# One transpose for lambda's real and imaginary rows, and two products without a reader removed

## The chip, the cores and the metric

The kernel runs on one core of a Trainium2 chip. The metric is the device time of one execution in microseconds (us), and the figure for a kernel is the median over several executions. A core has these engines, each with its own queue of instructions that it works through in order: PE (TensorE, matrix products; its weight loads are listed apart as PEld), DVE (VectorE), ACT (ScalarE), POOL (GpSimd), and SP (SyncE, which here only issues DMA transfers). An instruction waits on semaphores until what it reads has been written and what it overwrites has been read.

## The reference, cut to what matters

One encoder layer on 512 tokens of 1024 features, all in float32. A normalised input is projected by `w_in`; part of it feeds a state-space branch (S5), part a gated mixing branch (gMLP); the two are merged by sigmoid gates. Cross-attention to 256 memory tokens and a SwiGLU feed-forward network follow, each with a residual.

```python
def s5_scan(u, lam_re, lam_im, log_step, b_re, b_im, c_re, c_im, reverse):
    lam = lax.complex(lam_re, lam_im)                 # (32 groups, 64 states)
    step = jnp.exp(log_step)[:, None]
    lam_bar = jnp.exp(lam * step)
    b_bar = ((lam_bar - 1.0) / lam)[..., None] * b
    ...
def reference(...):
    n = rms_norm(h, mix_norm_g[i]); proj = n @ w_in[i]
    ya = s5_branch(xa, ...)                           # forward and backward direction
    yb = sgu_branch(zu, zv, ...)                      # layer_norm(gelu(zv)), position mixing
    h = h + (gate_a * (ya @ w_proj_a) + gate_b * (yb @ w_proj_b)) @ w_out
    h = h + memory_cross_attention(rms_norm(h, ...), memn, w_q, w_k, w_v, w_xo)
    h = h + swiglu(rms_norm(h, ...), w_gate, w_up, w_down)
```

The parameters `s5_lam_re` and `s5_lam_im` have the shape (direction, group, state) = 2 x 32 x 64.

## The kernel before, in words

Every large product is made of three matmuls. A float32 matrix is split into a high part (a cast on ACT, L85, the tile `whi`) and a low part (a subtraction on DVE, L86, the tile `wlo`), and high x high, high x low and low x high are summed in PSUM. Weights come as blocks of 128 x 1024 elements: an SP transfer into `wraw`, the cast, the subtraction, then the matmuls; each of the three kinds of tile has three buffers. Products of the input projection are the rows `pt` (zv, the gated branch) and `pf` (other columns). In attention and feed-forward a quadrant scheme with pre-added weights is used; its products are the rows of `product` (L1258).

The state-space branch is side work: a Python generator, `s5_program`, yields what each step costs, and a credit that grows with the main products (`tick`) decides where the next step's code is put between them. What this case touches of it, in its order:

- `s5_setup` (from L692). `lam` comes in as 32 rows of 128 values (two directions of 64 states) for the real and the same for the imaginary part, and is turned on PE to 128 x 32 (L710, tile `plam` in PSUM), then copied by DVE into a slab of small tiles (L712). The rows of B and C are turned in four groups of four transposes (`pbc`, L733 and L741), copied by ACT to `raw_b` and `raw_c`. From `lam` and the step come the decay (Exp, L750), the angle, its reduction (L751 to L756), two Sin on ACT (L757, L758), and the powers (L766 to L780).
- `s5_kernels` (from L861) makes on DVE the factors `e0`, `e1` and on PE the convolution taps: a group `pk` (L894, L899) of 32 + 32 matmuls in a pinned order, into one bank.
- `s5_inputs` (from L946) makes on DVE the input factors (L980 to L984), which are turned (`pw`, L959), copied to `wt` by ACT (L960, two halves) and multiplied with the inputs `u` (`pz`, L966); ACT and DVE keep half of the result each (L971, L972).

Beside it runs `layer_norm` (from L1140) of the four token tiles of zv: DVE makes the mean `nm` (L1143, L1144), ACT two sums of squares (L500), DVE the variance `ms` (L1148, L1149), POOL its power -1/2 (`r`, L1150), DVE the product `nm` (L1151) and ACT the normalised tile `zt` (L1152). POOL's queue also carries weight transfers (L289, `bsum`).

Three things set the order. The code is written in an order that the credit decides; then a scheduler reorders each engine's instructions at build time with a simulated timeline (`schedule_with_timeline_sim`, L2024); and instructions wrapped in `in_order` keep the order in which they were written among each other. Small results in PSUM take turns in three banks (`aux`); the large accumulations have five (`bank`). `idle_product` (L1262) writes a 128 x 512 product into an `aux` bank that nothing reads; it is called once in attention (L1576) and once in the feed-forward network (L1775), each time inside `in_order`.

Of the kernel before, what the change touches and what calls it, by code (L numbers as in the profile page):

```python
# [9 lines left out]
F32 = mybir.dt.float32  # L10
# [7 lines left out]
P = 128  # L18
# [8 lines left out]
G = 32  # L27
# [25 lines left out]
def hybrid_layer_kernel(  # L53
# [8 lines left out]
    nc = tc.nc  # L62
    x, mem, out = x[0], mem[0], out[0]
# [13 lines left out]
    def bank(name):  # L77
        return pm.tile([P, 512], F32, tag="mm", name=name)

    def aux(name, shape=(P, 512)):  # L80
        return pa.tile(list(shape), F32, tag="aux", name=name)
# [12 lines left out]
    in_order = tc.keep_in_program_order  # L94
# [395 lines left out]
    ident = cp.tile([P, P], F32, name="ident")  # L490
# [73 lines left out]
    def token_slot(name, place=NEAR):  # L564
        return tuple(slot(tag, (P, KD, T), F32R, name, place) for tag in "BC")
# [3 lines left out]
    s5p = s5.enter_context(tc.tile_pool(name="s5", bufs=1))  # L569
# [119 lines left out]
    V = nc.vector  # L689
    lo_, hi_ = slice(0, 64), slice(64, 128)  # L690

    def s5_setup():  # L692
        A_ = nc.scalar
        slab = s5p.tile([P, 32, G], F32, tag="wt", name="slab", bufs=2)
        used = [0]

        def small():
            used[0] += 1
            return slab[:, used[0] - 1, :]
# [2 lines left out]
        for d in range(2):  # L702
            nc.sync.dma_start(ls[64 * d:64 * d + 64, :], s5_log_step[0, d].partition_broadcast(64))
        in_order(A_.activation(stp, ls, AF.Exp))
        lam = []
        lrows = s5p.tile([G, 2, 2, 64], F32, tag="etmp", name="lrows")
        for i, src in enumerate((s5_lam_re, s5_lam_im)):
            nc.sync.dma_start(lrows[:, i], src[0].rearrange("d g p -> g d p"))
            ps = aux("plam", (P, G))
            nc.tensor.transpose(ps, lrows[:, i].rearrange("g d p -> g (d p)"), ident[:G, :G])  # L710
            l = small()
            V.tensor_copy(l, ps)  # L712
            lam.append(l)
        lr, li = lam
        yield 0.3


# [12 lines left out]
        for n in range(2):  # L730
            ps = aux("pbc", (P, C // 4, P))
# [6 lines left out]
        for i in range(2):  # L738
            ps = aux("pbc", (P, C // 4, P))
# [319 lines left out]
    def s5_program():  # L1059
        yield from s5_setup()  # L1060
        for o in (2, 3):
            yield from s5_kernels(o)
        while "u" not in st:
            yield None
        zh = s5p.tile([P, NCH, 2, G], F32, name="zh")
        st["zh"] = zh
        for o in range(NO):
            yield from s5_inputs(o)
        for o in (0, 1):
            yield from s5_kernels(o)  # L1070
        while st.get("nz", 0) < 2 * NO:
            yield None
        yield None
        yield from s5_scan()
        for _ in range(2):
            yield None
        for o in range(NO):
            yield from s5_outputs(o)
# [129 lines left out]
    for h in range(H):  # L1208
        ps = bank("psv")
# [49 lines left out]
                                     stop=k == 3 and i == 2, skip_group_check=True)  # L1259
        tick(2.7)  # L1260

    def idle_product(x, y):  # L1262

        in_order(nc.tensor.matmul(aux("idle"), x[:, 0, 0:P], y[:, 4, :], start=True, stop=True))

    def unit_bank(name):
        return bank(name).rearrange("p (j t) -> p j t", j=2)

    def seed(x):
        v = unit_bank("qv")  # L1270
        nc.scalar.copy(v, x)
        return v
# [147 lines left out]
    hn_hi, hn_lo = token_slot("hn", AWAY)  # L1420
# [53 lines left out]
    def v_evac(half):  # L1474
        def f(t, ps):
# [10 lines left out]
    hops = {q: (hn_hi[:, ks, ts], hn_lo[:, ks, ts])  # L1486
            for q, ks, ts in ((1, K0, T0), (2, K1, T0), (7, K0, T1), (4, K1, T1))}
# [85 lines left out]
    qx, qq_ = unit_bank("qx"), None  # L1573
    query_product(qx, 0, 1, True)
    qv = seed(qx)
    idle_product(hops[1][0], hn_hi)  # L1576
    qq_ = unit_bank("qq")
    query_product(qq_, 0, 5, True)
    query_product(qv, 0, 2)
# [40 lines left out]
    fn_hi, fn_lo = token_slot("fn", AWAY)  # L1620
# [3 lines left out]
    ps = {t: bank(f"pt{t}") for t in range(NT)}  # L1624
# [45 lines left out]
    held, ps = [], {}  # L1670
# [70 lines left out]
    ops = {1: fn_q(K0, T0), 2: fn_q(K1, T0), 7: fn_q(K0, T1), 4: fn_q(K1, T1)}  # L1741
# [14 lines left out]
    def unit_second(u, v):  # L1756
        product(v, u, 2, False, ops)
        put(u, 0, T0, v)
# [3 lines left out]
    ps = [bank("pf0"), bank("pf1")]  # L1762
# [9 lines left out]
    begun = unit_start(UNITS[0])  # L1772
    gate_part(1, T0)
    unit_second(UNITS[0], begun[1])
    idle_product(ops[1][0], fn_hi)  # L1775
    for i in range(2):
        gate_part(i, T1)
    for j in range(2):
# [51 lines left out]
    for i, u in enumerate(UNITS):  # L1830
        final = i == len(UNITS) - 1
        x, v = begun
# [196 lines left out]
```

## Time and profile before

| | us |
|---|---|
| median of 3 executions (lowest, highest) | 863.52 (862.94, 864.19) |
| the profiled execution | 863.27 |
| its span, first to last instruction | 861.5 |
| outside the span | 1.77 |
| PE busy | 854.4 (99%) |
| weight loads (PEld) busy, beside PE | 765.6 (89%) |
| DVE busy | 662.8 (77%) |
| ACT busy | 465.2 (54%) |
| POOL busy | 89.2 (10%) |

A row of a timeline shows the start in us from the span's start, the duration in us, the engine, the line in the kernel, the operation, out<-in, the shape, how often it stands in a row (xN), and in brackets how long the engine was idle before it and which instruction ended that. A matmul's duration includes the way through the array, so it overlaps the next one; what it costs is the distance from its start to the next start. Plain float32 matmuls (transposes, `pk`, `pz`) are recorded as two passes each, so a group of eight shows as x16; transposes show once.

### The profile page before, as it was taken

The numbers are of one execution on the slowest core, as the hardware profiler recorded it, in microseconds if no ns is written. First come the engines' busy times: TensorE is split into PE (matmuls) and PEld (weight loads), VectorE is DVE, ScalarE is ACT, GpSimd is POOL, SyncE is SP. The second block draws the span as 40 slices with busy tenths as digits, with TensorE's granted clock in tenths as the row PEclk, the third lists the DMA queues.
The fourth block names the chain that finished last, engine by engine and source line by source line (L and its number), as shares of the span: only waits on it lengthen the run. The fifth ranks groups of instructions, "written<-read, shape, count | busy, mean of one in ns | idle before, by whom it ended". The sixth has DMA issues, their size and how long they took to land.

```text
span 861.5 us, 14748 instructions
## 1 busy us (share of the span) xinstructions
PE 854.4 (99%) x5768; PEld 765.6 (89%) x5768; DVE 662.8 (77%) x1079; ACT 465.2 (54%) x698; POOL 89.2 (10%) x119
## 2 busy tenths in 40 slices
PE   9999999999999999999999999999999999999997
PEld 6888888888889988899899888999999999988886
DVE  7699989899646867678758755867877768899876
ACT  6744763244455544457547544645545454655674
POOL 0002201211021110010010001000211111000000
PEclk9999999999999999999999999999999999999999
DMA  9759567987475798635696555557899898366564
GB/s 267 215 170 316 124 196 163 237 219 191 133 221 159 247 313 256 224 109 197 215 278 160 141 144 150 147 159 192 206 240 228 216 224 226 99 185 213 184 198 162
DMA packets 116200, 170.61 MB, mean 198 GB/s; under 512 B 9489, under 2 KB 80801, under 8 KB 116002
## 3 DMA queue, kind: packets, MB, share of 16 engines
q1 hardware_dynamic: 95778, 140.51, 49.9%
q0 software_dynamic: 20064, 28.55, 20.6%
q8 instruction: 45, 0.74, 0.3%
q10 hardware_dynamic: 288, 0.61, 0.2%
q14 instruction: 25, 0.20, 0.1%
HBM read 160.75 MB, written 48.73 MB: 243 GB/s over the span
## 4 chain that ended last, share of the span: by engine, by line
PE 99%; DVE 0%; ACT 0%; issue 0%
PE pf L374 27%; PE pt L374 18%; PE px L1258 13%; PE pq L1258 6%; PE dx L374 5%; PE dq L374 5%; PE pv L1258 3%; PE bx L1258 3%; PE qx L1258 3%; PE dv L374 2%; PE pz L966 2%; PE qv L1258 1%; PE po L374 1%; PE psc L374 1%; PE py L1022 1%; PE qq L1258 1%
## 5 line engine op out<-in xcount | busy, mean ns | idle before, releaser
L85 ACT CAST whi<-wraw 128x1024 fp32r<-128x1024 f32 x141 | 145.3, 1030 | 157.7 <-PE pf L374 52.3
L86 DVE TENSOR_TENSOR wlo<-wraw,whi 128x1024 fp32r<-128x1024 f32 x141 | 168.0, 1194 | 56.3 <-ACT whi L85 55.8
L374 PE MATMUL pf<-xn,whi 128*128 128x512 f32 x448 | 139.9, 392 | 0.0
L374 PEld LDWEIGHTS pf<-xn,whi 128*128 128x128 f32 x448 | 83.6, 188 | 17.2 <-issue 0.2
L374 PE MATMUL pf<-xn,wlo 128*128 128x512 f32 x224 | 87.7, 391 | 0.0
L1258 PE MATMUL px<-fn,whi 128*128 128x256 f32 x480 | 83.5, 277 | 0.0
L1258 PEld LDWEIGHTS px<-fn,whi 128*128 128x128 f32 x480 | 72.5, 188 | 0.2
L86 DVE TENSOR_TENSOR wlo<-b,whi 128x1024 fp32r<-128x1024 f32 x40 | 48.9, 1222 | 26.0 <-ACT whi L85 26.0
L85 ACT CAST whi<-b 128x1024 fp32r<-128x1024 f32 x40 | 42.2, 1054 | 47.9 <-PE px L1258 27.7
L1258 PE MATMUL px<-fn,wlo 128*128 128x256 f32 x240 | 66.4, 277 | 0.0
L1258 PE MATMUL pq<-s,whi 128*128 128x256 f32 x320 | 55.0, 276 | 0.0
L86 DVE TENSOR_TENSOR wlo<-t,whi 128x1024 fp32r<-128x1024 f32 x30 | 36.7, 1224 | 19.5 <-ACT whi L85 19.5
L85 ACT CAST whi<-t 128x1024 fp32r<-128x1024 f32 x30 | 31.6, 1054 | 36.2 <-PE pv L1258 13.3
L374 PEld LDWEIGHTS pf<-xn,wlo 128*128 128x128 f32 x224 | 42.1, 188 | 8.6
L1258 PEld LDWEIGHTS pq<-s,whi 128*128 128x128 f32 x320 | 48.1, 188 | 0.0
L1258 PEld LDWEIGHTS px<-fn,wlo 128*128 128x128 f32 x240 | 45.1, 188 | 0.0
L374 PE MATMUL pt<-whi,xn 128*128 128x512 f32 x128 | 44.4, 405 | 0.0
L1258 PE MATMUL pq<-s,wlo 128*128 128x256 f32 x160 | 44.2, 276 | 0.0
L374 PE MATMUL dx<-whi,s 128*128 128x512 f32 x132 | 41.4, 390 | 0.0
L374 PE MATMUL dq<-whi,s 128*128 128x512 f32 x122 | 38.1, 389 | 0.0
L289 POOL DMA_DIRECT2D dsum<-in_w_down_dram x12 | 13.2, 1103 | 171.2 <-DMA dsum<-in_w_down_dram 167.6
L500 ACT ACTIVATE sq<-h 128x512 f32<-128x512 f32 x23 | 14.5, 630 | 29.3 <-DVE h L1448 24.1
(458 smaller groups left out, 2243.3 us busy)
## 6 DMA issues: line engine op xcount, KB each, us to landing
wraw<-in_w_in_dram SPq DMA_DIRECT2D x34, 512.0 KB, 4.8
dsum<-in_w_down_dram SPq DMA_DIRECT2D x20, 512.0 KB, 6.0
wraw<-dsum SPq DMA_DIRECT2D x20, 512.0 KB, 3.9
b<-in_w_gate_dram SPq DMA_DIRECT2D x15, 512.0 KB, 6.2
b<-in_w_up_dram SPq DMA_DIRECT2D x15, 512.0 KB, 5.1
wraw<-in_w_down_dram SPq DMA_DIRECT2D x15, 512.0 KB, 4.5
dsum<-in_w_down_dram POOLq DMA_DIRECT2D x10, 512.0 KB, 7.7
dsum<-dsum POOLq DMA_DIRECT2D x10, 512.0 KB, 8.7
```

What stands on the lines that cost most here:

```text
L85: hi = nc.scalar.copy(dst_hi, src)
L86: lo = nc.vector.tensor_tensor(dst_lo, src, dst_hi.bitcast(F32), ALU.subtract)
L289: plan[j + step][1].append((0, lambda d=dst, x=more: nc.gpsimd.dma_start(d, x, accum_op=ALU.add)))
L374: m = nc.tensor.matmul(ps, a[x], b[y], start=start and i == 0, stop=stop and i == 2, skip_group_check=free)
L500: act = nc.scalar.activation(sq[:, :src.shape[-1]], src, AF.Square, bias=bias, accum_out=dst)
L966: nc.tensor.matmul(ps[:, g, :], wt[:, g, :], u[:, o * GO + g, :], start=True, stop=True)
L1022: in_order(nc.tensor.matmul(ps[64 * j:64 * j + 64, :, :, h, :].rearrange("p q d c -> p d q c"), a, b, start=k == ks[0], stop=k == ks[2], t ...
L1258: nc.tensor.matmul(ps[:, j, :], a[x], b[y], start=start and j == k == i == 0, stop=k == 3 and i == 2, skip_group_check=True)
```

## The change

First, the two parts of `lam` are loaded below each other into one tile of 64 rows x 128 values, turned by one transpose to 128 x 64 and copied by one DVE instruction into two neighbouring small tiles. The two transfers stay, with the same sizes. Second, `idle_product` and its two calls go.

```diff
--- before.py
+++ after.py
@@ -702,16 +702,13 @@
         for d in range(2):
             nc.sync.dma_start(ls[64 * d:64 * d + 64, :], s5_log_step[0, d].partition_broadcast(64))
         in_order(A_.activation(stp, ls, AF.Exp))
-        lam = []
-        lrows = s5p.tile([G, 2, 2, 64], F32, tag="etmp", name="lrows")
+        lrows = s5p.tile([2 * G, 2, 64], F32, tag="etmp", name="lrows")
         for i, src in enumerate((s5_lam_re, s5_lam_im)):
-            nc.sync.dma_start(lrows[:, i], src[0].rearrange("d g p -> g d p"))
-            ps = aux("plam", (P, G))
-            nc.tensor.transpose(ps, lrows[:, i].rearrange("g d p -> g (d p)"), ident[:G, :G])
-            l = small()
-            V.tensor_copy(l, ps)
-            lam.append(l)
-        lr, li = lam
+            nc.sync.dma_start(lrows[G * i:G * i + G], src[0].rearrange("d g p -> g d p"))
+        ps = aux("plam", (P, 2, G))
+        nc.tensor.transpose(ps.rearrange("p i g -> p (i g)"), lrows.rearrange("r d p -> r (d p)"), ident[:2 * G, :2 * G])
+        lr, li = small(), small()
+        V.tensor_copy(slab[:, used[0] - 2:used[0], :], ps)
         yield 0.3
 
 
@@ -1259,10 +1256,6 @@
                                      stop=k == 3 and i == 2, skip_group_check=True)
         tick(2.7)
 
-    def idle_product(x, y):
-
-        in_order(nc.tensor.matmul(aux("idle"), x[:, 0, 0:P], y[:, 4, :], start=True, stop=True))
-
     def unit_bank(name):
         return bank(name).rearrange("p (j t) -> p j t", j=2)
 
@@ -1573,7 +1566,6 @@
     qx, qq_ = unit_bank("qx"), None
     query_product(qx, 0, 1, True)
     qv = seed(qx)
-    idle_product(hops[1][0], hn_hi)
     qq_ = unit_bank("qq")
     query_product(qq_, 0, 5, True)
     query_product(qv, 0, 2)
@@ -1772,7 +1764,6 @@
     begun = unit_start(UNITS[0])
     gate_part(1, T0)
     unit_second(UNITS[0], begun[1])
-    idle_product(ops[1][0], fn_hi)
     for i in range(2):
         gate_part(i, T1)
     for j in range(2):
```

The lines after the first place are numbered 3 lower in the changed kernel, those behind the removed function lower still. The numbers behind names (buffers) shift by 3 as well.

Since the scheduler works over the whole program, the order of each engine differs in many places between 25 and 110 us, and in few behind. Three of them are shown, first before and then after the change.

ACT in the setup of the state-space branch (`slab` holds the small tiles: rows L704, L750/L747 are Exp, L757/L758 and L754/L755 the Sin; `raw_b` and `raw_c` are the copies of the turned B and C). Before:

```order
L704 ACTIVATE slab_337<-slab_337 128x32
L750 ACTIVATE slab_337<-slab_337 128x32
L85 CAST whi_381<-wraw_191 128x1024
L85 CAST whi_466<-wraw_379 128x1024
L734 COPY raw_b_360<-pbc_361 128x4x2x64
L734 COPY raw_b_360<-pbc_373 128x4x2x64
L85 CAST whi_472<-wraw_464 128x1024
L742 COPY raw_c_391<-pbc_392 128x4x128
L757 ACT_TABLE_LOAD
L757 ACTIVATE slab_337<-slab_337 128x32
L758 ACTIVATE slab_337<-slab_337 128x32
L1097 ACT_TABLE_LOAD
```

After:

```order
L704 ACTIVATE slab_337<-slab_337 128x32
L747 ACTIVATE slab_337<-slab_337 128x32
L754 ACT_TABLE_LOAD
L754 ACTIVATE slab_337<-slab_337 128x32
L755 ACTIVATE slab_337<-slab_337 128x32
L85 CAST whi_378<-wraw_191 128x1024
L731 COPY raw_b_357<-pbc_358 128x4x2x64
L85 CAST whi_463<-wraw_376 128x1024
L731 COPY raw_b_357<-pbc_370 128x4x2x64
L739 COPY raw_c_388<-pbc_389 128x4x128
L85 CAST whi_469<-wraw_461 128x1024
L739 COPY raw_c_388<-pbc_395 128x4x128
```

The load of the Sin table and the two Sin have moved ahead of three casts of weight blocks and the copies of B and C.

PE at the second group of convolution taps (`pt` are products of the input projection, `pk` the taps, `pw` turned input factors), the two parts before:

```order
L374 MATMUL pt2_783<-wlo_704,xn_137 128x512
L374 MATMUL pt2_783<-whi_703,xn_138 128x512
L894 MATMUL pk_741<-e0_613,bd0_519 32x128 x4
L374 MATMUL pt3_784<-whi_703,xn_137 128x512
L374 MATMUL pt3_784<-wlo_704,xn_137 128x512
```

```order
L374 MATMUL pt0_781<-whi_788,xn_138 128x512
L894 MATMUL pk_741<-e1_695,bd1_520 32x128 x4
L899 MATMUL pk_741<-e0_613,bd0_519 16x16 x4
L899 MATMUL pk_741<-e1_695,bd1_520 16x16 x4
L894 MATMUL pk_741<-e0_613,bd0_519 32x128 x4
L894 MATMUL pk_741<-e1_695,bd1_520 32x128 x4
L899 MATMUL pk_741<-e0_613,bd0_519 16x16 x4
L899 MATMUL pk_741<-e1_695,bd1_520 16x16 x4
L959 MATMUL pw_877<-ident_95,wsx_336 128x128 x4
```

After:

```order
L374 MATMUL pt1_779<-whi_700,xn_138 128x512
L891 MATMUL pk_738<-e0_610,bd0_516 32x128 x4
L891 MATMUL pk_738<-e1_692,bd1_517 32x128 x4
L896 MATMUL pk_738<-e0_610,bd0_516 16x16 x4
L896 MATMUL pk_738<-e1_692,bd1_517 16x16 x4
L891 MATMUL pk_738<-e0_610,bd0_516 32x128 x4
L891 MATMUL pk_738<-e1_692,bd1_517 32x128 x4
L896 MATMUL pk_738<-e0_610,bd0_516 16x16 x4
L896 MATMUL pk_738<-e1_692,bd1_517 16x16 x4
L374 MATMUL pt1_779<-whi_700,xn_137 128x512
L374 MATMUL pt1_779<-wlo_701,xn_137 128x512
```

The group stood in two parts with nine `pt` products between them, and stands in one piece now.

ACT where the layer norm and the inputs of the state-space branch meet (`squares` are the sums of squares, `zt` with L1097/L1094 the Gelu of zv, with L1152/L1149 the normalised tile, `wt` the turned factors, `zh` the kept halves of `pz`). Before:

```order
L500 ACTIVATE squares_1026,ss_1083<-zt_334,nm_1082 128x512 x2
L500 ACTIVATE squares_1026,ss_1131<-zt_334,nm_1130 128x512 x2
L1097 ACTIVATE zt_334,zsum_335<-pt2_783 128x512
L85 CAST whi_904<-wraw_895 128x1024
L960 COPY wt_975<-pw_976 128x512
L960 COPY wt_975<-pw_982 128x512
L971 COPY zh_829<-pz_988 64x8x64
L1097 ACTIVATE zt_334,zsum_335<-pt3_784 128x512
L85 CAST whi_1039<-wraw_902 128x1024
L1152 ACTIVATE zt_334<-zt_334,nm_1082,r_1085 128x1024
L1152 ACTIVATE zt_334<-zt_334,nm_1130,r_1133 128x1024
L971 COPY zh_829<-pz_1013 64x8x64
```

After:

```order
L500 ACTIVATE squares_1023,ss_1128<-zt_334,nm_1127 128x512
L1094 ACTIVATE zt_334,zsum_335<-pt2_780 128x512
L1149 ACTIVATE zt_334<-zt_334,nm_1079,r_1082 128x1024
L85 CAST whi_901<-wraw_892 128x1024
L957 COPY wt_972<-pw_973 128x512
L500 ACTIVATE squares_1023,ss_1223<-zt_334,nm_1222 128x512 x2
L957 COPY wt_972<-pw_979 128x512
L1149 ACTIVATE zt_334<-zt_334,nm_1127,r_1130 128x1024
L968 COPY zh_826<-pz_985 64x8x64
L1094 ACTIVATE zt_334,zsum_335<-pt3_781 128x512
L85 CAST whi_1036<-wraw_899 128x1024
L1149 ACTIVATE zt_334<-zt_334,nm_1222,r_1225 128x1024
```

The first `zt` of L1149, which waits for POOL's first `r`, now stands ahead of the cast of `whi_901` and of the two halves of `wt_972` (before: behind the corresponding `whi_904` and `wt_975`, and behind `whi_1039`).

PE's user of that `wt`, before:

```order
L374 MATMUL pf0_1035<-xn_138,whi_897 128x512
L374 MATMUL pf0_1035<-xn_137,wlo_898 128x512
L374 MATMUL pf0_1035<-xn_137,whi_897 128x512
L966 MATMUL pz_1013<-u_543,wt_975 128x64 x8
L374 MATMUL pf0_1035<-xn_138,whi_897 128x512
```

After:

```order
L374 MATMUL pf0_1032<-xn_138,whi_894 128x512
L374 MATMUL pf0_1032<-xn_137,wlo_895 128x512
L963 MATMUL pz_1010<-u_540,wt_972 128x64 x4
L374 MATMUL pf0_1032<-xn_137,whi_894 128x512
L374 MATMUL pf0_1032<-xn_138,whi_894 128x512
L374 MATMUL pf0_1032<-xn_137,wlo_895 128x512
L374 MATMUL pf1_1033<-xn_137,whi_894 128x512
L963 MATMUL pz_1010<-u_540,wt_972 128x64 x4
L374 MATMUL pf1_1033<-xn_138,whi_894 128x512
```

The group `pz` that reads it stood in one piece behind five `pf` products, and stands in two halves behind nine now.

## The prediction

> **What bounds the kernel now.** I read the page first, then PE's waits, then PE's timeline at each place that the change touches, then what feeds PE there. The page:
>
> ```profile
> PE 854.4 (99%) x5768; PEld 765.6 (89%) x5768; DVE 662.8 (77%) x1079; ACT 465.2 (54%) x698; POOL 89.2 (10%) x119
> ...
> PEclk9999999999999999999999999999999999999999
> ...
> PE 99%; DVE 0%; ACT 0%; issue 0%
> ```
>
> All waits of PE in the whole execution:
>
> ```profile
> PE pt L577 <- DVE ones L493: 1.1, 1, 1.1
> PE ptr L639 <- issue: 0.2, 1, 0.2
> PE ptr L639 <- DVE ms L622: 0.2, 1, 0.2
> ```
>
> PE carries 99% of the chain of waits, and its three waits (1.5 us) lie in the start. Everything behind is one unbroken row of matmuls at a constant granted clock, so two things move the time: PE work that is taken out counts in full, and every new wait of PE counts in full. DVE, ACT and POOL matter only where they make PE wait.
>
> **The two products without a reader.** PE's timeline at both places:
>
> ```profile
> 428.72 0.40 PE L1264 MATMUL idle<-hn 128*128 128x512 f32 x1
> 428.96 0.40 PE L1258 MATMUL qq<-hse,whi 128*128 128x256 f32 x2
> ...
> 548.91 0.39 PE L1264 MATMUL idle<-fn 128*128 128x512 f32 x1
> 549.14 1.07 PE L374 MATMUL pf<-fn,s 128*128 128x256 f32 x8
> ```
>
> From start to next start they cost 0.24 and 0.23 us: -0.47. They fill no gap: the products behind them (`qq`, `pf`) have no wait in the list above and their operands are weights and activations of long before, so nothing slides into the hole. In the feed-forward network the new order also puts five products of `w_up` ahead of a unit product; this only swaps equal work. Bounds: 0 (if the next product had needed those 0.23 us) to -0.47; I take -0.47.
>
> **The transposes of lambda.** PE around the first, and the transfers that feed both:
>
> ```profile
> 23.67 0.40 PE L374 MATMUL pt<-whi,xn 128*128 128x512 f32 x1
> 24.00 0.24 PE L710 MATMUL plam<-ident,lrows 32*128 32x32 f32 x1
> 24.17 0.50 PE L374 MATMUL pt<-whi,xn 128*128 128x512 f32 x1
> 24.51 0.39 PE L374 MATMUL pt<-wlo,xn 128*128 128x512 f32 x1
> 24.74 0.63 PE L374 MATMUL pt<-whi,xn 128*128 128x512 f32 x2
> ```
>
> ```profile
> L708 SPq DMA_DIRECT2D lrows<-in_s_lam_im_dram x1: 327/327/327, 9.3 to 9.3; - x1
> DMA to landing us min/median/max: 7.4/7.4/7.4
> ```
>
> A 512-column matmul takes 0.23 (24.51 to 24.74). From 23.67 to 24.51 there are two of them and one transpose: 0.84 - 0.46 = 0.38 for the transpose, most of it the two changes of kind, not its columns. The joint one has 64 columns instead of 32: its columns are part of the 0.17 from 24.00 to 24.17, so at most 0.17 more (0.55), at least nothing more (0.38). Two at 0.38 go, one comes: -0.38 to -0.21; I take -0.37, since nearly all of the 0.38 lies in the neighbours. It needs both transfers, but the later one was issued at 9.3 and lands by 16.7, and the transpose keeps its place at about 24.0: no wait.
>
> **What the new order does on PE.** The second group of taps `pk` stood in two parts and stands in one. PE at the two parts, and at a group in one piece:
>
> ```profile
> 71.01 0.39 PE L374 MATMUL pt<-whi,xn 128*128 128x512 f32 x1
> 71.33 0.42 PE L894 MATMUL pk<-e,bd 128*32 128x128 f32 x8
> 71.68 0.50 PE L374 MATMUL pt<-whi,xn 128*128 128x512 f32 x1
> 72.02 0.39 PE L374 MATMUL pt<-wlo,xn 128*128 128x512 f32 x1
> ...
> 73.63 0.39 PE L374 MATMUL pt<-whi,xn 128*128 128x512 f32 x1
> ...
> 74.94 1.09 PE L959 MATMUL pw<-ident,wsx 128*128 128x128 f32 x8
> ...
> 145.42 0.61 PE L374 MATMUL pf<-xn,whi 128*128 128x512 f32 x2
> ...
> 147.17 0.50 PE L374 MATMUL pf<-xn,wlo 128*128 128x512 f32 x1
> 147.51 0.62 PE L374 MATMUL pf<-xn,whi 128*128 128x512 f32 x2
> ```
>
> Part one: 72.02 - 71.01 - 0.46 = 0.55. Part two: 74.94 - 73.63 - 0.23 = 1.08. Whole: 147.51 - 145.42 - 3 x 0.23 = 1.40. Saved: 0.23. Elsewhere about as many groups `pz` and `pw` are split as are joined; at 0.1 per change of kind (0.34 instead of 0.23 at 147.17) I take 0, with 0.2 to either side.
>
> PE work in all: -0.47 - 0.37 - 0.23 = -1.07 us.
>
> **What the new order does to the feeders.** The two Sin and their table now stand ahead of the casts. Two idle times of DVE come from the old order, a third from a store:
>
> ```profile
> 33.67 1.23 DVE L86 TENSOR_TENSOR wlo<-wraw,whi 128x1024 fp32r<-128x1024 f32 x1 [1.37 <-ACT whi L85]
> ...
> 36.20 0.22 DVE L769 TENSOR_TENSOR pows<-slab 128x32 f32<-128x32 f32 x1 [1.31 <-ACT slab L757]
> ...
> 79.51 1.22 DVE L870 TENSOR_TENSOR e<-raw_c,pe 128x1024 f32<-128x1024 f32 x1 [1.38 <-DMA ed<-e]
> ```
>
> ```profile
> 27.91 1.05 ACT L85 CAST whi<-wraw 128x1024 fp32r<-128x1024 f32 x1 [1.88 <-PE pt L374]
> ```
>
> ACT was idle for 1.88 before its cast at 27.91; the table and the Sin fit about there, so the casts are not late for PE, and DVE gains 1.37 + 1.31 = 2.68 us. By itself that is worth nothing, since DVE is off the path. But DVE's lead lets the scheduler put the layer norm forward, and there is an operation that takes long once:
>
> ```profile
> L1150 POOL TENSOR_TENSOR r<-ms,mhalf x4: 542/548/3804, 91.6 to 107.6; 128x1 f32<-128x1 f32 x4
> ```
>
> ```profile
> 87.73 1.17 POOL L289 DMA_DIRECT2D bsum<-in_w_proj_b_dram  x1 [3.47 <-DMA bsum<-in_w_proj_b_dram]
> 91.61 4.33 POOL L1150 TENSOR_TENSOR r<-ms,mhalf 128x1 f32<-128x1 f32 x2 [2.71 <-DVE ms L1149]
> ...
> 95.45 0.16 DVE L1151 TENSOR_TENSOR nm<-nm,r 128x1 f32<-128x1 f32 x1 [0.46 <-POOL r L1150]
> ```
>
> ```profile
> 86.24 0.71 ACT L500 ACTIVATE squares<-zt,nm 128x512 f32<-128x512 f32 x1
> ...
> 88.93 1.03 ACT L85 CAST whi<-wraw 128x1024 fp32r<-128x1024 f32 x1
> 89.87 1.05 ACT L960 COPY wt<-pw 128x512 f32<-128x512 f32 x2
> ...
> 95.65 2.38 ACT L1152 ACTIVATE zt<-zt,nm,r 128x1024 f32<-128x1024 f32 x2 [1.98 <-DVE nm L1151]
> ```
>
> ```profile
> 92.36 1.89 PE L966 MATMUL pz<-u,wt 128*128 128x64 f32 x16
> ...
> 98.74 1.04 PE L959 MATMUL pw<-ident,wsx 128*128 128x128 f32 x8
> ```
>
> POOL's first `r` takes 3.80 us, the others 0.55. Before, ACT copied the two halves of `wt` at 89.87, and the first `zt` stood behind them, at 95.65. Now `zt` stands ahead of a cast and of both `wt` halves that PE's next `pz` reads. When does that `r` start? DVE has one sum of 1.14 us, a few small rows and one copy less ahead of it (1.3), and 2.68 of idle time less: 91.61 - 4.0 = 87.6. If the 1.38 at 79.51 goes too, 86.2. The transfer ahead of it on POOL (87.73 to 88.90) must have moved as well; paced by the same lead of about 2 us it ends near 86.9, and I take 86.9. Then `zt` starts 4.04 later (91.61 to 95.65), takes 1.19, the cast 0.94, the half `wt` 0.57: ready at 93.6 (92.9 to 94.3). PE reaches its `pz` after four more 512-column products and less the 0.60 saved till then: 92.36 + 0.91 - 0.60 = 92.7. New wait: 0.2 to 1.6, and 0.9 by the start that I take. The second half of `wt` follows 2.0 later (two squares at 0.71 and a copy), and PE's second half 1.8 later: no further wait of note. DVE stands still behind its `nm` for about 2.6 us, with two sums and a low part queued behind it; that eats the lead, and the `pw` that reads them is due only at 98.7.
>
> The Trainium skill, "GPSIMD Engine Reference", Instruction dispatch, puts the first call of a freshly loaded POOL kernel at approximately 6 us above its normal time. By that figure, as an estimate, `r` would take 2.7 us longer than the row says and the time would come to about 865.9; the trace has 3.80 for it, and that is used.
>
> **The sum.** -1.07 + 0.9 = -0.17 against the profiled 863.27, so 863.1; the profiled execution lies 0.25 below the median of the runs: 863.3 as a median.
>
> **Rivals.**
> 1. No new wait: `r` starts by 85.9, or the scheduler's order leaves ACT in time. -1.07: 862.4. For it: PE had no wait anywhere behind the start. Against it: 3.80 us now stand ahead of a copy that had 2.5 us of slack (89.87 to 92.36).
> 2. Slower, by the same `r`: if DVE's lead does not reach the layer norm (the 2.68 are lost again at the store of 79.51 or behind POOL's transfers), `r` starts only 1.2 earlier, at 90.4, and `wt` comes at 97.1: PE waits 4.4, +3.3, 866.8. It decides from a start at 88.8, where the wait passes 2.8. For it: POOL's transfer before had itself waited 3.47. The Trainium skill, "TensorE: Matmul & The Clock Gate", The HAM clock gate, has the TensorE clock halved after an idle window of about 3.4 us; by that, as an estimate, such a wait would be followed by some 3.4 us at half speed, +1.7, and no run here shows it, since the granted clock has no slice below 9 tenths. The removed products fill no gap, so at their own places it cannot start.
> 3. The removed work was hidden and nothing changes: 863.5. Against it: PE's starts follow each other without a gap.
>
> **How the numbers follow.** A difference under 0.2% (1.7 us) is about what a measurement cannot tell from none. My forecast (waits of 0.2 to 1.6) 0.50; rival 1 0.22; rival 3 0.04; rival 2 0.16; other new waits in the reordered stretch from 25 to 110 us, for +2 to +3 in all, 0.08. Faster by 1.7 needs more than all the PE work that I can find, so only a lucky spread of rival 1 (runs lie 0.6 apart) gets there: 0.08. Slower: 0.16 and three quarters of 0.08, 0.22. Same: 0.70. The range goes from 861.8 (rival 1 less the spread) to 865.5, which leaves rival 2 out and takes the smaller new waits in; the likeliest alone has 862.6 to 864.1.
>
> **What would show it.** In the changed kernel: no `idle` rows, one `plam` row; start-to-start across it 0.38 to 0.55 above the two matmuls; `pk` at 65 to 75 us with one part less; first `r` near 86.9 and again about 3.8 long; in PE's waits one new line `pz` <- ACT `wt` of about 0.9 near 93. A list as short as before means rival 1; `pz`, `pw` or `pf` lines over 2.8 us together mean rival 2. The prediction is wrong if PE work fell by another sum than about 1.1, or if waits arise anywhere outside 84 to 110 us.

## The result

The changed kernel took 869.92 us (median of 6, 868.61 to 872.76), the kernel before beside it 863.8 (median of 6, 862.94 to 866.37): a ratio of 1.0071, 95% interval 1.0054 to 1.0088. It is slower by some 6 us. Forecast were 863.3, with a range up to 865.5 and a chance of 0.22 for slower.

The page of the changed kernel, the lines that answer to those shown of before:

```profile
PE 860.9 (99%) x5765; PEld 772.7 (89%) x5765; DVE 663.7 (76%) x1078; ACT 464.5 (53%) x698; POOL 86.0 (10%) x119
...
PEclk9999999999999999999999999999999999999999
...
PE 93%; DMA 3%; DVE 2%; ACT 1%; issue 0%; POOL 0%; SPq 0%; ACTq 0%; DVEq 0%
```

All waits of PE in it (line, what for: total us, times, longest):

```profile
PE pt L577 <- DVE ones L493: 1.1, 1, 1.1
PE pt L374 <- DVE wlo L86: 0.3, 1, 0.3
PE ptr L639 <- DVE xt L633: 0.3, 1, 0.3
PE ptr L639 <- issue: 0.2, 1, 0.2
PE ptr L639 <- DVE ms L622: 0.2, 1, 0.2
```

The waits grew by 0.6 us. PE has three instructions less (5765 against 5768), and is busy 6.5 us longer (860.9 against 854.4) at the same granted clock. So it is not waits: the same products take longer. (That the chain leaves PE for 7% means only that it was followed back through the 0.3 us wait for a weight block.) Groups of PE's products between 549 and 742 us, first before, then after:

```profile
L1258 PE MATMUL px<-fn,whi 128*128 128x256 f32 x432 | 74.5, 276 | 0.0
L1258 PE MATMUL px<-fn,wlo 128*128 128x256 f32 x216 | 59.6, 276 | 0.0
```

```profile
L1255 PE MATMUL px<-fn,whi 128*128 128x256 f32 x432 | 77.3, 281 | 0.0
L1255 PE MATMUL px<-fn,wlo 128*128 128x256 f32 x216 | 60.7, 281 | 0.0
```

The second number from the end is the mean duration in ns: every group of 256-column products of this stretch has 281 where it had 276. Where that begins is seen at the place of the removed product. PE there, before:

```profile
548.20 0.40 PE L1258 MATMUL pv<-fn,whi 128*128 128x256 f32 x2
548.44 0.28 PE L1258 MATMUL pv<-fn,wlo 128*128 128x256 f32 x1
...
548.91 0.39 PE L1264 MATMUL idle<-fn 128*128 128x512 f32 x1
549.14 4.13 PE L374 MATMUL pf<-fn,s 128*128 128x256 f32 x35
```

And after:

```profile
548.98 0.40 PE L1255 MATMUL pv<-fn,whi 128*128 128x256 f32 x2
549.21 0.28 PE L1255 MATMUL pv<-fn,wlo 128*128 128x256 f32 x1
549.33 3.93 PE L374 MATMUL pf<-fn,s 128*128 128x256 f32 x32
```

Before the product, one 256-column product follows the other after 0.118 us (548.20 to 548.91 for six; two rows are left out). Behind it the step is (4.13 - 0.28) / 34 = 0.113 us. Without it, the step stays (3.93 - 0.28) / 31 = 0.118. Some 1,700 such products stand between 549 and 742 us (1,703 in PE's list). Over the whole stretch the mean step is 113.3 ns before (549.14 to 742.26, 1,704 steps) and 117.8 after (549.33 to 749.44, 1,699 steps), and 1,704 x 0.0044 = 7.5 us. That is more than the whole loss; the rest of the change had gained something. In the text below the two are called the 113 step and the 118 step.

### The profile page after: what moved, and what is told of

Its sections match the earlier page's. It is cut to its first block, busy times and chain, and to the rows that moved or that the text cites. A ratio compares the mean times of both kernels' runs of the same rounds, so it can differ in the third digit from the quotient of the medians.

```text
span 868.6 us, 14740 instructions
## 1 busy us (share of the span) xinstructions
PE 860.9 (99%) x5765; PEld 772.7 (89%) x5765; DVE 663.7 (76%) x1078; ACT 464.5 (53%) x698; POOL 86.0 (10%) x119
## 4 chain that ended last, share of the span: by engine, by line
PE 93%; DMA 3%; DVE 2%; ACT 1%; issue 0%; POOL 0%; SPq 0%; ACTq 0%; DVEq 0%
PE pf L374 23%; PE pt L374 16%; PE px L1255 13%; PE pq L1255 7%; PE dx L374 5%; PE dq L374 5%; PE pv L1255 3%; PE bx L1255 3%; PE qx L1255 3%; PE dv L374 2%; DMA wraw<-in_w_out_dram 2%; PE pz L963 2%; PE qv L1255 1%; PE po L374 1%; PE psc L374 1%; PE py L1019 1%
## 5 line engine op out<-in xcount | busy, mean ns | idle before, releaser
L1255 PE MATMUL px<-fn,whi 128*128 128x256 f32 x480 | 86.2, 281 | 0.0
L1255 PE MATMUL pq<-s,whi 128*128 128x256 f32 x320 | 57.0, 281 | 0.0
```

The lines of the kernel that those rows point to most:

```text
L1255: nc.tensor.matmul(ps[:, j, :], a[x], b[y], start=start and j == k == i == 0, stop=k == 3 and i == 2, skip_group_check=True)
```

## The experiments

**Each part alone.** First, the changed kernel with the feed-forward product put back; second, the kernel before without only that product; third, without only the attention product; fourth, the kernel before with only the joint transpose. The edits, of the first against the changed kernel and of the others against the kernel before:

```diff
# feed-forward product back
     unit_second(UNITS[0], begun[1])
+    idle_product(ops[1][0], fn_hi)
# feed-forward product gone
-    idle_product(ops[1][0], fn_hi)
# attention product gone
-    idle_product(hops[1][0], hn_hi)
# lambda only: the first hunk of the change
```

> The changed kernel with the feed-forward product without a reader put back (same place, 512 columns), nothing else. Theory A (this product switches the following row of 256-column products from 118 to 113 ns per product, some 1700 of them): 862.5 to 863.2, slots of 113 ns from about 549 us on. Theory B (the new order in the state-space stretch and its late weights cost the time): stays at 869 to 870, slots whatever they are. Theory C (each of the two products keeps a part of PE quick): about half way, 866.

Measured: 863.23 us (12 executions) against 864.6 (31 executions of the kernel before), ratio 0.9985, interval 0.9965 to 1.0006.

> The kernel before with only the feed-forward product without a reader taken out. Theory A: 870.5 to 871.5 (863.8 - 0.2 + 7.5), slots of 118 ns from 549 us on. Theory B: 863.5. Theory C: 866 to 867.

Measured: 872.47 us (6) against the same 864.6, ratio 1.0082, interval 1.0055 to 1.0108. (The ratios here are those on record; they differ a little from the quotient of the two medians, which is 1.0091 here.)

> The kernel before with only the attention product without a reader taken out. Theory A: 863.5, since PE's slots at its place are 113 ns before it and behind it. Theory B: 863.5. Theory C: 866 to 867.

Measured: 863.89 us (12), ratio 0.9986, interval 0.9969 to 1.0003.

> The kernel before with only the joint transpose of lambda (and the order that follows from it). Theory A: 863.0 to 863.4 (863.8 - 0.37 - 0.23, less what small waits take). Theory B: 869 to 870, since the whole reordering of the state-space stretch comes with this part. Theory C: 863.2.

Measured: 863.05 us (12), ratio 0.9982, interval 0.996 to 1.0003.

The feed-forward product alone carries the loss, in both directions: back in, the 6 us are gone; taken out of the kernel before, 8 us appear. The attention product and the joint transpose with its whole new order cost nothing; all three kernels that keep the feed-forward product lie 0.14% to 0.18% below the kernel before, with intervals that just reach past 1. Theories B and C fall. PE between 560 and 740 us in the second of them shows the same groups as in the changed kernel:

```profile
L1258 PE MATMUL px<-fn,whi 128*128 128x256 f32 x426 | 76.3, 281 | 0.0
```

and in the first as before:

```profile
L1255 PE MATMUL px<-fn,whi 128*128 128x256 f32 x432 | 74.5, 276 | 0.0
```

**What about the product does it.** Three kernels with the product back, but 384, 256 and 128 columns wide, one execution each:

```diff
-        in_order(nc.tensor.matmul(aux("idle"), x[:, 0, 0:P], y[:, 4, :], start=True, stop=True))
+        in_order(nc.tensor.matmul(aux("idle")[:, :n], x[:, 0, 0:P], y[:, 4, 0:n], start=True, stop=True))
```

> As the kernel with the feed-forward product put back, but 384 columns wide instead of 512. Theory A1 (the product works because it lasts longer than a weight load, so that the next load gets ahead of its matmul): slots of 113 ns from 549 us on, about 863. Theory A2 (any product more at this place shifts the phase): 113 ns too. Theory A3 (only a full bank of 512 columns does it): 118 ns, about 870.

> The same with 256 columns, the width of its neighbours. A1: 118 ns from 549 us on, about 870, since it lasts no longer than the others. A2: 113 ns, about 863. A3: 118 ns, about 870.

> The same with 128 columns. A1: 118 ns from 549 us on, about 870; a shorter product lets the loader fall further behind. A2: 113 ns, about 863. A3: 118 ns, about 870.

Measured: 862.34, 869.81 and 862.3 us (the kernel before beside them: 867.25, one execution, so only the steps are compared). PE behind the product of 384, of 256 and of 128 columns, in this order:

```profile
547.94 0.34 PE L1261 MATMUL idle<-fn 128*128 128x384 f32 x1
548.12 4.13 PE L374 MATMUL pf<-fn,s 128*128 128x256 f32 x35
```

```profile
548.11 0.28 PE L1261 MATMUL idle<-fn 128*128 128x256 f32 x1
548.23 4.05 PE L374 MATMUL pf<-fn,s 128*128 128x256 f32 x33
```

```profile
548.03 0.22 PE L1261 MATMUL idle<-fn 128*128 128x128 f32 x1
548.09 3.08 PE L374 MATMUL pf<-fn,s 128*128 128x256 f32 x25
```

4.13 for 35 is the 113 step, 4.05 for 33 the 118 step. The 25 products behind the narrow one begin with some at the longer step and go over within a microsecond (3.08 - 0.28 = 2.80 for 24, which is 0.117 on average, with one long step at the start); the groups behind have 276 ns. All three theories were wrong as put: it is not the length (128 does it too), not one product more (256 does not do it), not the full bank (384 does it). What works at this place is a product of another width than its neighbours; the one of 256 columns, written to PSUM in the same way, changes nothing.

**Does the state hold, and does the place matter?** The product of 512 columns, after the two parts of the gate product that follow:

```diff
     for i in range(2):
         gate_part(i, T1)
+    idle_product(ops[1][0], fn_hi)
```

> The product of 512 columns, but four parts of the gate product later (48 products of 256 columns and more behind its old place). If the state holds until something switches it: 118 ns up to the new place and 113 ns behind it up to about 742 us, 0.2 to 0.4 us more than with the old place, about 863.5. If the old place itself mattered: 118 ns throughout, about 870.

Measured: 864.91 us in one execution, with 1.0 us of waits of `pz` for ACT in it. PE at the new place:

```profile
554.82 1.34 PE L374 MATMUL pf<-fn,s 128*128 128x256 f32 x10
556.00 0.39 PE L1261 MATMUL idle<-fn 128*128 128x512 f32 x1
556.23 0.39 PE L374 MATMUL pf<-fn,whi 128*128 128x256 f32 x2
556.46 0.28 PE L374 MATMUL pf<-fn,wlo 128*128 128x256 f32 x1
556.57 0.39 PE L374 MATMUL pf<-fn,whi 128*128 128x256 f32 x2
```

Up to the product the step is (1.34 - 0.28) / 9 = 0.118, and behind it three products take 0.34 (556.23 to 556.57), 0.113 each. The step holds over hundreds of products until something switches it, and the old place is not special.

**Without a wasted product.** The changed kernel with the first 256-column product of the second half of the gate computed as two of 128; a sum of the same terms, nothing unread.

```diff
+                if cut and j == 0 and k == 0:
+                    for h in (slice(tsl.start, tsl.start + P), slice(tsl.start + P, tsl.stop)):
+                        nc.tensor.matmul(ps[j][:, h], hi[:, k, cs], act[0][:, kk, h], start=False, stop=False, ...)
```

> The changed kernel without any product that nothing reads, but with one useful product of 256 columns of the gate part computed as two of 128. The scheduler puts one of the halves about 27 products ahead (into the slow stretch behind the last transposes) and the other where the removed product stood. Theory A4 (a product of another width breaks the rhythm, and the row settles in the quick step): 113 ns from the first half on, still 113 ns behind the second, about 862.3. Theory A5 (every break toggles between the two steps): 113 ns between the halves and 118 ns behind the second, about 870.

Measured: 869.45 us (4) against 863.63 (17), ratio 1.0087, interval 1.0056 to 1.0119. PE around both halves:

```profile
543.23 1.10 PE L374 MATMUL pf<-fn,s 128*128 128x256 f32 x8
544.17 0.22 PE L412 MATMUL pf<-fn,s 128*128 128x128 f32 x1
...
546.80 0.39 PE L1263 MATMUL pv<-fn,whi 128*128 128x256 f32 x2
547.03 0.28 PE L1263 MATMUL pv<-fn,wlo 128*128 128x256 f32 x1
547.14 0.39 PE L1263 MATMUL pv<-fn,whi 128*128 128x256 f32 x2
...
547.48 0.22 PE L412 MATMUL pf<-fn,s 128*128 128x128 f32 x1
547.54 0.45 PE L415 MATMUL pf<-fn,s 128*128 128x256 f32 x2
547.83 2.40 PE L374 MATMUL pf<-fn,s 128*128 128x256 f32 x19
```

Ahead of the first half the step is (1.10 - 0.28) / 7 = 0.117, between the halves 0.34 for three, and behind the second (2.40 - 0.28) / 18 = 0.118. The second break undid the first. So a break does not set the row to the better step; these two toggled it.

That is no general rule. The attention product of 512 columns is a break, too, in a row at the 113 step, and it leaves the row there. PE at it, in the kernel before:

```profile
428.38 0.39 PE L1258 MATMUL qx<-hn,whi 128*128 128x256 f32 x2
428.61 0.28 PE L1258 MATMUL qx<-hn,wlo 128*128 128x256 f32 x1
428.72 0.40 PE L1264 MATMUL idle<-hn 128*128 128x512 f32 x1
...
429.31 0.39 PE L1258 MATMUL qq<-hse,whi 128*128 128x256 f32 x2
429.54 0.28 PE L1258 MATMUL qq<-hse,wlo 128*128 128x256 f32 x1
429.65 0.39 PE L1258 MATMUL qq<-hse,whi 128*128 128x256 f32 x2
```

Three products take 0.34 us ahead of it (428.38 to 428.72) and 0.34 behind it (429.31 to 429.65). It is the same in the three other kernels that keep this product. Whether the width makes the difference (128 columns switched a quick row, 512 did not) or something else was not tested.

Another question is whether each narrow product counts or each departure from the row's width. The last two kernels ask it: the two halves next to each other (with that stretch of PE pinned), and the kernel before with two products of 512 columns instead of one.

```diff
# halves together: both halves and the products of the unit ahead in in_order(...)
# two products, on the kernel before:
     idle_product(ops[1][0], fn_hi)
+    idle_product(ops[1][0], fn_hi)
```

> As the kernel with the split useful product, but both halves of 128 columns stand next to each other, where the removed product stood (that stretch of PE is pinned). Theory A5a (each change of width away from the row and back counts once, however many products stand between): 113 ns from there on, 862 to 863. Theory A5b (every narrow product toggles the step, so two toggle it back): 118 ns behind them, about 870.

> The kernel before with two products of 512 columns that nothing reads in the feed-forward network, next to each other, instead of one. Theory A5a: 113 ns behind them, 0.23 us more than before, 863.5 to 864. Theory A5b: 118 ns behind them, about 871.

Measured: 862.91 us (10) against 863.31 (13), ratio 0.9987, interval 0.9972 to 1.0001; and 864.51 in one execution (with 1.2 us of waits of `pw` for DVE). Both have the 113 step from there on; PE between 560 and 740 us, the halves together and then the two products:

```profile
L1263 PE MATMUL px<-fn,whi 128*128 128x256 f32 x432 | 74.5, 276 | 0.0
```

```profile
L1258 PE MATMUL px<-fn,whi 128*128 128x256 f32 x432 | 74.5, 276 | 0.0
```

Two halves next to each other act as one departure: they switch the row from the 118 step and do not switch it back. The kernel with two products of 512 columns says less, since a product of 512 columns left the attention row, which was quick already, at the 113 step as well. The kernel with the halves together computes nothing that is not read, and its row is at the 113 step.

**The 384-column product, timed.** One execution could have had the 113 step by chance, so this kernel was run twelve times:

> The changed kernel with a feed-forward product without a reader of 384 columns (as in the look before), now timed. Quick step from 548 us on in every execution: 862.3 to 863.5 against the kernel before, 0.05% to 0.2% less; if the quick step came by chance in the one look, some executions near 870.

Measured: 863.0 us (12, 860.96 to 868.12) against 863.63 (17), ratio 0.9999, interval 0.9982 to 1.0015. The slowest execution, 868.12, is the profiled one, and it has the 113 step (the changed kernel's fastest took 868.61), so the step did not come by chance. This execution, with a span of 866.3 us, shows the kind of wait that the prediction had forecast. PE's longest wait in it, and POOL and ACT ahead of it:

```profile
PE pz L963 <- ACT wt L957: 3.0, 1, 3.0
```

```profile
91.05 1.17 POOL L289 DMA_DIRECT2D bsum<-in_w_proj_b_dram  x1 [7.57 <-DMA bsum<-in_w_proj_b_dram]
91.71 1.11 POOL L1147 TENSOR_TENSOR r<-ms,mhalf 128x1 f32<-128x1 f32 x1
...
93.05 1.24 ACT L1149 ACTIVATE zt<-zt,nm,r 128x1024 f32<-128x1024 f32 x1 [6.92 <-DVE nm L1148]
...
95.13 0.57 ACT L957 COPY wt<-pw 128x512 f32<-128x512 f32 x1
```

The wait cost more than its 3.0 us. The granted clock of this execution is 0.50 from 95.25 to 102.08 us and 1.00 on both sides, which also shows in the fifth of the 40 slices of its page:

```profile
PEclk9999899999999999999999999999999999999999
```

The same kernel had no such wait in the single execution above, whose span is 860.5. Against that one, PE's products start 0.2 us later ahead of the wait, 3.3 later at its end, and 6.3 later when the clock is back at 1.00. So the half clock cost another 3.0 us. It shows in two more profiled executions: for 6.83 us behind a wait of 1.7 us (feed-forward product back) and for 3.41 us behind one of 2.3 us (attention product gone). Behind single waits of up to 1.2 us no run has it (the first microseconds of the kernel aside).

## Why the prediction was wrong

**The step that failed: "They fill no gap", -0.47 for both products without a reader.** For the attention product it held: PE's step is 0.113 ahead of its place and behind it in both kernels, and without it the time is 0.9986 of before, which fits -0.24 us but does not prove it. For the feed-forward product -0.23 should have been +7.5 - 0.2: PE's busy time rose by 6.5 us where the prediction had PE's work fall by 1.07. I priced the product by its own slot and looked for a wait behind it; I did not compare the slots of its neighbours on the two sides. The evidence was in the fence of the prediction: `549.14 1.07 ... x8` is (1.07 - 0.28) / 7 = 0.113 per product, while the `pv` rows just ahead, which I did not quote, have 0.118. A product that nothing reads and that fills no gap, at a place where the step changes, should have been a rival with the price of 1,704 x 0.0044 = 7.5 us. With it the sum closes for the two profiled executions: 7.5 for the step, -0.23 for the slot, -0.84 as forecast for the other PE work and 0.6 of waits are 7.0, and the span grew by 7.1 (868.6 against 861.5).

**Rival 3** had the removed work hidden, and rival 2 the loss in the state-space stretch. None of the rivals had the mechanism; that slower got 0.22 was for another reason.

**The transposes of lambda: right.** The joint one costs, in the changed kernel,

```profile
23.60 0.40 PE L374 MATMUL pt<-whi,xn 128*128 128x512 f32 x1
23.92 0.27 PE L709 MATMUL plam<-ident,lrows 64*128 64x64 f32 x1
24.13 0.50 PE L374 MATMUL pt<-whi,xn 128*128 128x512 f32 x1
24.46 0.40 PE L374 MATMUL pt<-wlo,xn 128*128 128x512 f32 x1
```

0.86 - 0.46 = 0.40 (forecast 0.38 to 0.55), so 0.36 were saved, and it waited for nothing. The group of taps now stands in one piece, as the order said, and costs 1.40 (68.50 to 70.36, less two products of 0.23), as forecast.

**The new wait of `pz`, 0.9 us: not in the profiled execution, but real in others.** The first `r` took 1.11 us there, not 3.80: I had taken one execution's figure for a property of the operation. In all other profiled executions of this study it took 1.11 to 1.53, so the 3.80 was the exception. The Trainium skill's 6 us for a first call ("GPSIMD Engine Reference", Instruction dispatch) are seen in none of them. The first `r` started 1.5 us later than forecast (88.36 against 86.9), but it was 2.7 shorter. The two errors together made `wt` 1.2 us earlier than forecast, which is more than the wait of 0.9: ACT had its first half of `wt` at 91.78 + 0.57, just ahead of PE's `pz` at 92.76.

```profile
91.78 0.57 ACT L957 COPY wt<-pw 128x512 f32<-128x512 f32 x1
```

```profile
92.76 1.00 PE L963 MATMUL pz<-u,wt 128*128 128x64 f32 x8
```

With 0.4 us to spare it depends on when POOL's transfer ahead of `r` may start: of the ten profiled kernels with this order six had no such wait, the others 0.4, 0.7, 1.7 and 3.0 us. That is the mechanism of rival 2, whose start of 90.4 the execution above passed (91.71), with its price of 4.4 too high by the 2.7 us that `r` was shorter (4.4 - 2.7, plus 1.3 for the later start, is the 3.0). The prediction named +1.7 us for a halved clock behind such a wait, as an estimate that no run showed then, and by a rule with 3.4 us of idle time. The half clock is seen now, behind shorter waits, and where it can be compared it cost 3.0 us. So "every new wait of PE counts in full" was too little: the wait of 3.0 us cost some 6. Kernels with the old order have such waits elsewhere (2.3 us of `pw` for DVE in the kernel without the attention product). Such waits add to the spread of the single executions of both kernels; they do not make the difference between them, since the two profiled executions compared here have none over 1.1 us and the step differs all the same.

**The other PE work, -0.84 without the feed-forward product's 0.23,** has the right sign and size as far as it can be seen: the three kernels that keep that product lie 0.7 to 1.6 us below the kernel before, each with an interval that reaches to no gain.

**A rule beside the row.** PE's step in this row is 113 or 118 ns for a product of 256 columns. The Trainium skill, "TensorE: Matmul & The Clock Gate", Back-to-back issue gap, says that in a row of weight loads and matmuls the spacing is set by both, pipelined; by its formula for a single matmul one of 256 columns takes about 109 ns, as an estimate. By the Trainium skill's formula on the same page, LDWEIGHTS (loading the stationary operand), a load of 128 columns takes about 107 ns, as an estimate. Both steps of this row lie above the two figures, so the trace does not contradict it. But that page of the Trainium skill has one spacing per width, and here the same row has two, 4% apart.

**What stays open.** What in PE holds the two steps is not shown. Nor is there a rule for what switches it, and "a departure toggles" is not one: the attention product leaves its row at 113. In the kernel before, the row is at the 113 step up to 742.26, a block of 512-column products follows, and then the 118 step; the next such block (747.96 to 750.68) leaves it at 118. In the kernel with only the joint transpose the first of these blocks is followed by the 113 step after four products. Groups of transposes switch it in both directions (at about 541 to 113, at about 544 to 118), and those at about 462 leave it at 113.

## What to carry to other kernels

Before an instruction that looks useless is priced at its own length, compare the distances between starts ahead of it and behind it: if they differ, it may be what changes them, and the price at stake is that difference times everything that follows in the row. Taking out that one instruction alone, and putting it back alone, shows whether it is. On an engine that is 99% busy, look for a few ns per instruction in the largest groups before looking for waits, since 4.4 ns in each of 1,700 products outweigh every wait in these runs. A wait can cost twice its length: look at the granted clock behind it. And an extreme duration that stands once in one execution is a sample, not a cost; take a second execution before a forecast rests on it.

## What the runs showed of the hardware

A dense row of 256-column float32r products, each with its own load of 128 x 128 weights, runs at one of two steady steps, 113 or 118 ns from start to start, at the same granted clock (both profiled executions have 0.999), and stays in it over hundreds of products and across different operands and PSUM banks. One departure to another width (128, 384 or 512 columns, one product or two in a row) at the three places in the feed-forward network that were tried switched from the 118 to the 113 step in all eleven profiled executions that had one, and a product of the same 256 columns did not. In a row at the 113 step one of 128 columns switched back to 118 (one profiled execution), and one of 512 columns in attention left it at 113 (four). An explicit product of 128 or 384 columns that nothing reads, or a useful product cut into two neighbouring halves, was enough here, so the step could be chosen without wasted work. With no rule for the switches this holds for this order of products only, and the step has to be read from the trace again after every change of order.

Behind single waits of PE of 1.7, 2.3 and 3.0 us the granted clock was 0.50 for 6.83, 3.41 and 6.83 us; behind single waits of up to 1.2 us, the first microseconds of the kernel aside, it stayed at 1.00. The wait of 3.0 us so cost some 6.
